# TensorE kept in the source's order through an attention stage, with one head's last products moved between the next head's scores

## The chip, the cores and the metric

The kernel runs on one core of a Trainium2 chip. The metric is device time in microseconds (us) of one execution. Three runs of the kernel before the change took 1217.46, 1221.15 and 1222.93 us; the median, 1221.15 us, is the time that is compared.

## The reference

One decoder layer over 1024 positions of width 1024: RMSNorm and one input projection, whose columns feed a short gated convolution, a stick-breaking attention and a chunked spatial gating; an output projection; a squared-ReLU MLP of width 4096; a gated per-layer embedding. The change touches the attention alone:

```
q = rms_norm(q, q_norm_g); k = rms_norm(k, k_norm_g)      # 8 heads of 64
for each block of 128 queries:
    z = q k^T / 8;  causal = key < query
    log_beta = log_sigmoid(z);  log_rem = where(causal, log_sigmoid(-z), 0)
    suffix = reverse cumulative sum of log_rem over keys, without the key itself
    weights = where(causal, exp(log_beta + suffix), 0)
    o = weights v
```

The kernel takes the suffix as a running product: rem = sigmoid(-z) is scanned from the last key to the first, and the weight is sigmoid(z) times the scanned rem of the next key.

## The kernel before, in words

Every float32 product is done as three products of rounded parts (hi by hi, hi by lo, lo by hi). A part pair is made by `split`: ScalarE writes the hi part, VectorE the rest (lo).

The heads are worked in four pairs. `project(pr)` makes one pair's q, k and v: for each of 8 blocks t of 128 positions, 24 matmuls into one of two banks of the pool `ps_mm` (tile `qkv_ps`), then the chain that empties the bank: ScalarE's squares (`qk_sq`), VectorE's sum (`ss`), GpSimd's power (`rs`), VectorE's scaling of q and k (`qk`), ScalarE's hi part of v, VectorE's lo part of v. `turn_qk`, put off by `later`, transposes q and k of two blocks through a bank of `ps_tr` (3 banks) and splits them into QS, KH, KL.

`attend(pr)` has two generators for a step (head hh, group g of two query blocks t = 2g, 2g+1). `stick` makes the weights: for each t, one or two banks of `ps_z` (2 banks) of scores (tile `z`, up to 512 keys each), ScalarE's two sigmoids of each bank (`rem`, `wt`), VectorE's scan of `rem` over (t+1)*128 keys, and the product into `wt` (VectorE for t = 3, 5, 7, GpSimd else). `gather` multiplies them with v: per turn j, up to four transposes into a bank of `ps_tr` (`w_tr`), a split into `wT_hi` and `wT_lo`, and four matmuls into `av`; a turn's products come two turns after its transposes. `attention` runs `stick` of step i+1 and then `gather` of step i. The groups go 0, 1, 2, 3 for the first head of a pair and 3, 2, 1, 0 for the second, so that two steps with g = 3, the widest, follow each other in the middle of each pair.

`weave` draws alternately on `attention` and on a filler (`project` of the next pair, and with the last pair the convolution), by shares of units. The text order is not the order on the engines: the program is built with a scheduler that goes by estimated times and may issue any ready instruction of any engine ahead of others that it estimates late. Within an engine the order is then fixed, and semaphores are waited for in that order. `tc.issue_after(ins)` is a context that keeps what is written inside it behind `ins` on the engine of `ins`; it puts no wait into the program.

Of the kernel before, what the change touches and what calls it, by code (L numbers as in the profile page):

```python
# [32 lines left out]
def hybrid_block(ctx: ExitStack, tc: tile.TileContext, a: dict):  # L33
# [98 lines left out]

    last_hi, last_power = [None], [None]
# [27 lines left out]
    def product(ps, terms, first=True, last=True):  # L161


        for i, ((lh, ll), (rh, rl)) in enumerate(terms):
            nc.tensor.matmul(ps, lh, rh, start=first and i == 0, stop=False)  # L165
            nc.tensor.matmul(ps, lh, rl, start=False, stop=False)  # L166
            done = nc.tensor.matmul(ps, ll, rh, start=False, stop=last and i == len(terms) - 1)  # L167
        return done
# [16 lines left out]
    def mean_square(acc, s):  # L185


        ps = bank(ps_tr, "ms_ps")
        for t in range(4):
            nc.tensor.matmul(ps[:, 2 * t:2 * t + 2], acc[:, t * P:(t + 1) * P], ones[:, :2],  # L190
                             start=True, stop=True)
        ms = small.tile([P, 4], F32, tag=f"ms{s}", name=name("ms"), bufs=1)
        nc.vector.tensor_scalar(out=ms, in0=ps.rearrange("p (t two) -> p t two", two=2)[:, :4, 0],
                                scalar1=1.0 / D, scalar2=EPS, op0=ALU.mult, op1=ALU.add)
        r = small.tile([P, 4], F32, tag=f"r{s}", name=name("r"), bufs=1)
        power_mhalf(r, ms, 4)
        return ms, r

    def spread(r, R):

        diag = slot("diag", shape=(P, 4, P))
        nc.vector.tensor_tensor(
            out=diag, in0=ident.unsqueeze(1).broadcast_to([P, 4, P]),
            in1=r.unsqueeze(2).broadcast_to([P, 4, P]), op=ALU.mult)
        ps = bank(ps_tr, "R_ps")
        nc.tensor.matmul(ps, ones, diag.rearrange("p t c -> p (t c)"), start=True, stop=True)
        nc.scalar.copy(R, ps)
        return R
# [58 lines left out]
    def weave(first, first_total, second, second_total):  # L267


        done = [0, 0]  # L270
        while True:
            if done[0] * second_total <= done[1] * first_total:
                got = next(first, None)
                if got is None:
                    return
                done[0] += got
            else:
                done[1] += next(second, 1000)
# [57 lines left out]

    last_pool, last_act = [None], [None]
# [5 lines left out]
    def project(pr):  # L343
# [11 lines left out]
        for t in range(KT):  # L355
# [11 lines left out]
            for k0 in range(0, KT, 2):  # L367
# [3 lines left out]

            sq = half_tmp("qk_sq", (P, 4, HD + 1))
            nc.scalar.copy(sq[:, :, HD], ms1e[t].broadcast_to([P, 4]))
            nc.scalar.activation(sq[:, :, :HD], ps[:, :256].rearrange("p (h d) -> p h d", d=HD),
                                 AF.Square, scale=HD ** -0.5)
            ss = small.tile([P, 4], F32, tag="ss", name=name("ss"))
# [9 lines left out]
            if t % 2 == 0:  # L386
                V[t // 2] = slot("V", F32R, (P, 2, 2, 2, HD))
            v = V[t // 2][:, t % 2]
            split(ps[:, 256:].rearrange("p (h d) -> p h d", d=HD), v[:, :, 0], v[:, :, 1], scale=r1[t])
# [3 lines left out]
    def turn_qk(head, t, qk):  # L393

        QS, KH, KL, _, low_q = head
        th = t // 4
        tr = bank(ps_tr, "qk_tr")
        for i in range(2):
            for j in range(2):
                o = j * 256 + i * P  # L400
                nc.tensor.transpose(tr[:, o:o + P], qk[:, i, j * P:(j + 1) * P], ident)
        ws = slice((t % 4 - 1) * P, (t % 4 + 1) * P)

        split(tr[:, :256], QS[0][th][:, ws], low_q[th][:, ws], scale=gq)
        nc.scalar.activation(KH[0][th][:, ws], tr[:, 256:], AF.Copy, scale=gk)
        for hh, own in enumerate((lo_p, hi_p)):
            nc.vector.scalar_tensor_tensor(out=KL[hh][th][own, ws], in0=tr[own, 256:],
                                           scalar=gk[own], in1=KH[0][th][own, ws],
                                           op0=ALU.mult, op1=ALU.subtract)
# [11 lines left out]
    def attend(pr):  # L421
# [13 lines left out]
        def stick(hh, g):  # L435
            weights[hh, g] = []
            for t in (2 * g, 2 * g + 1):
# [5 lines left out]
                for kh in reversed(range(th + 1)):  # L443
# [3 lines left out]
                    nc.tensor.matmul(z, QS[hh][th][:, ts], KH[hh][kh][:, :n],  # L447
                                     start=True, stop=False)
                    nc.tensor.matmul(z, QS[hh][th][:, ts], KL[hh][kh][:, :n],
                                     start=False, stop=kh < th)  # L450
                    if kh == th:

                        nc.tensor.matmul(z[:, n - P:], ident_r, below, start=False, stop=True)
# [15 lines left out]
        def gather(hh, g):  # L469
# [5 lines left out]
            def turn(j):  # L475
# [4 lines left out]
                for kb in (2 * j, 2 * j + 1):  # L480
                    first = 0 if kb <= 2 * g else 1
                    parts.append((kb, n, first))
                    for i in range(first, 2):
                        nc.tensor.transpose(tr[:, n:n + P], wts[i][:, kb * P:(kb + 1) * P], ident)  # L484
# [6 lines left out]
            for j in range(-2, g + 1):  # L491
                if j + 2 <= g:
                    turned.append(turn(j + 2))
                    yield 2 * turned[-1][3] + 10
                if j < 0:
                    continue
                parts, hi, lo, _ = turned.pop(0)
                for kb, o, first in parts:
                    m = 256 - first * P
                    lhs = V[kb // 2][:, kb % 2, hh].rearrange("p two d -> p (two d)")  # L500
                    for part in (hi, lo):
                        nc.tensor.matmul(av[:, first * P:], lhs, part[:, o:o + m],  # L502
                                         start=kb == 0 and part is hi,
                                         stop=kb == 2 * g + 1 and part is lo)
                yield 8

            if yb is None:
                if both[0] is None:
                    both[0] = slot("y_both")
                t = both[0]  # L510
                nc.scalar.copy(t[:, (g % 2) * 256:(g % 2 + 1) * 256], av)
                if len(seen_g) % 2:
                    nc.gpsimd.dma_start(t[:HD], t[HD:], accum_op=ALU.add)
                    summed.append((y_dram[pr, g // 2, own], t))
                    both[0] = None
                seen_g.append(g)
                return
            low = half_tmp("av_lo")
            nc.scalar.copy(low[:HD], av[HD:])
            nc.vector.tensor_tensor(out=yb[g // 2][own, (g % 2) * 256:(g % 2 + 1) * 256],  # L520
                                    in0=av[:HD], in1=low[:HD], op=ALU.add)
# [3 lines left out]
    def attention():  # L525
# [5 lines left out]
        yield from parts[0][0](*steps[0][1:])  # L531
        for i, (pr, *step) in enumerate(steps):
            if i + 1 < len(steps):
                nxt, *ahead = steps[i + 1]
                if nxt not in parts:
                    parts[nxt] = attend(nxt)
                yield from parts[nxt][0](*ahead)
# [4 lines left out]
            if i % 2 == 1:  # L542
                parts[pr][2]()
# [12 lines left out]
    def gating():  # L556
# [26 lines left out]
        def turn_c(th, j, yc, y):  # L583
            tr = bank(ps_tr, "c_tr")
            for t in range(4):
                nc.tensor.transpose(tr[:, t * P:(t + 1) * P],
# [756 lines left out]
```

## Time and profile before

| | |
|---|---|
| median of three runs | 1221.15 us |
| the profiled execution | 1216.81 us, its span 1214.9 us |
| TensorE busy | 1191.8 us (98% of the span) |
| VectorE, ScalarE, GpSimd busy | 886.8, 629.1, 400.9 us |
| mean granted TensorE clock | 0.993 |

PE is TensorE, PEld its weight loads, DVE VectorE, ACT ScalarE, POOL GpSimd. In tables of windows each row is a stretch of the span with its length, each engine's busy time in it (in brackets the number of instructions), the granted TensorE clock as a share of full speed, and the use of the DMA engines. A matmul's record is longer than the step to the next one, since matmuls are pipelined: a busy PE is not yet a PE at its peak.

### The profile page before, as it was taken

Reading aid. Unit: us, or ns where it says so; the run is one execution under the profiler, and the core shown is the slowest. Engines: PE = TensorE matmul, PEld = TensorE weight load, DVE = VectorE, ACT = ScalarE, POOL = GpSimd, SP = SyncE. Lnnn points to the kernel's source line nnn. Section 1 sums busy time; section 2 is a strip of 40 time slices with the busy share of each in tenths; the row PEclk is TensorE's granted clock in tenths of the full one; section 3 lists DMA queues with packets and bytes.
Section 4 is the critical chain, followed back from the end, with each engine's and each line's share of the span. In section 5 each row is a group of like instructions: output and inputs, shape, how many; then the busy total and the mean of one; then the engine's idle time right before and its main releaser. Section 6 shows DMA issues by size and latency. Waiting matters only on the chain.

```text
span 1214.9 us, 17743 instructions
## 1 busy us (share of the span) xinstructions
PE 1191.8 (98%) x5852; PEld 1018.2 (84%) x5852; DVE 886.8 (73%) x1310; ACT 629.1 (52%) x1244; POOL 400.9 (33%) x408
## 2 busy tenths in 40 slices
PE   9999899999999999999999999999999999999997
PEld 7899899898988888888888888888888888888886
DVE  7846888988887657877878768787665556753597
ACT  7736767667764355744333333356443444546542
POOL 3324345365343312124453544421023301013412
PEclk9999999999999999999999999999999999999998
DMA  9602359999554786779999899778889985654857
GB/s 318 222 18 94 124 166 267 247 184 171 132 116 101 164 287 207 198 194 269 251 256 251 231 261 258 217 249 277 321 248 313 279 264 171 217 163 112 179 160 208
DMA packets 127964, 254.04 MB, mean 209 GB/s; under 512 B 14496, under 2 KB 22432, under 8 KB 127168
## 3 DMA queue, kind: packets, MB, share of 16 engines
q1 hardware_dynamic: 94992, 168.08, 41.8%
q0 software_dynamic: 27664, 57.05, 25.0%
q10 hardware_dynamic: 5216, 27.79, 6.4%
q8 instruction: 46, 0.75, 0.2%
q14 instruction: 46, 0.38, 0.1%
HBM read 192.30 MB, written 92.80 MB: 235 GB/s over the span
## 4 chain that ended last, share of the span: by engine, by line
PE 86%; DVE 5%; DMA 4%; POOL 1%; issue 1%; ACT 1%; SPq 0%; ACTq 0%; DVEq 0%; POOLq 0%
PE f_ps L812 25%; PE d_ps L812 25%; PE g_ps L812 6%; PE qkv_ps L165 3%; PE qkv_ps L166 3%; PE qkv_ps L167 3%; PE av L502 2%; PE w_tr L484 2%; DVE rem L459 1%; PE vu_ps L167 1%; PE vu_ps L166 1%; PE vu_ps L165 1%; PE o_ps L167 1%; PE o_ps L165 1%; PE o_ps L166 1%
## 5 line engine op out<-in xcount | busy, mean ns | idle before, releaser
L139 DVE TENSOR_TENSOR w_lo<-raw,w_hi 128x512 fp32r<-128x512 f32 x280 | 245.1, 879 | 88.1 <-ACT w_hi L138 86.4
L138 ACT CAST w_hi<-raw 128x512 fp32r<-128x512 f32 x280 | 171.9, 619 | 232.6 <-PE d_ps L812 112.6
L812 PE MATMUL f_ps<-hn_hi,w_hi 128*128 128x512 f32 x448 | 175.1, 392 | 0.0
L812 PE MATMUL d_ps<-f_hi,w_hi 128*128 128x512 f32 x448 | 174.8, 390 | 0.0
L812 PE MATMUL f_ps<-hn_lo,w_hi 128*128 128x512 f32 x448 | 174.7, 390 | 0.0
L812 PE MATMUL f_ps<-hn_hi,w_lo 128*128 128x512 f32 x448 | 174.5, 390 | 0.0
L812 PE MATMUL d_ps<-f_hi,w_lo 128*128 128x512 f32 x448 | 174.3, 389 | 0.0
L812 PE MATMUL d_ps<-f_lo,w_hi 128*128 128x512 f32 x448 | 174.3, 389 | 0.0
L459 DVE TENSOR_TENSOR_SCAN rem<-rem 128x128 f32<-128x128 f32 (+3 forms) x64 | 90.2, 1420 | 23.0 <-ACT rem L454 22.9
L812 PEld LDWEIGHTS f_ps<-hn_lo,w_hi 128*128 128x128 f32 x448 | 84.4, 188 | 17.9 <-issue 0.2
L812 PEld LDWEIGHTS f_ps<-hn_hi,w_hi 128*128 128x128 f32 x448 | 84.5, 189 | 17.6 <-issue 0.2
L812 PEld LDWEIGHTS f_ps<-hn_hi,w_lo 128*128 128x128 f32 x448 | 84.4, 188 | 17.7
L812 PEld LDWEIGHTS d_ps<-f_hi,w_hi 128*128 128x128 f32 x448 | 84.1, 188 | 17.7 <-issue 0.2
L812 PEld LDWEIGHTS d_ps<-f_lo,w_hi 128*128 128x128 f32 x448 | 84.1, 188 | 17.6 <-issue 0.2
L812 PEld LDWEIGHTS d_ps<-f_hi,w_lo 128*128 128x128 f32 x448 | 84.1, 188 | 17.5
L165 PE MATMUL qkv_ps<-whi,xn_hi 128*128 128x384 f32 x256 | 90.4, 353 | 0.1
L167 PE MATMUL qkv_ps<-whi,xn_lo 128*128 128x384 f32 x256 | 87.8, 343 | 0.0
L166 PE MATMUL qkv_ps<-wlo,xn_hi 128*128 128x384 f32 x256 | 87.6, 342 | 0.0
L139 DVE TENSOR_TENSOR f_lo<-raw,f_hi 128x512 fp32r<-128x512 f32 x112 | 77.0, 718 | 12.6 <-ACT f_hi L138 12.2
L138 ACT CAST f_hi<-raw 128x512 fp32r<-128x512 f32 x112 | 67.0, 620 | 28.9 <-DMA raw<-f_dram 25.9
L798 POOL TENSOR_TENSOR S<-S,sq 128x512 f32<-128x512 f32 x19 | 27.4, 1440 | 157.8 <-ACT sq L874 157.8
L174 POOL TENSOR_TENSOR rs<-ss,mhalf 128x4 f32<-128x4 f32 x32 | 40.1, 1253 | 83.1 <-DVE ss L377 83.1
(252 smaller groups left out, 2704.4 us busy)
## 6 DMA issues: line engine op xcount, KB each, us to landing
raw<-in_w_ff SPq DMA_DIRECT2D x148, 256.0 KB, 4.1
raw<-f_dram SPq DMA_DIRECT2D x112, 256.0 KB, 5.1
raw<-w_sums SPq DMA_DIRECT2D x64, 256.0 KB, 3.9
f_dram<-f SPq DMA_DIRECT2D x48, 256.0 KB, 4.0
f_dram<-t SPq DMA_DIRECT2D x48, 256.0 KB, 3.7
w_sums<-in_w_ff POOLq DMA_DIRECT2D x8, 1024.0 KB, 11.6
w_sums<-w_sums POOLq DMA_DIRECT2D x8, 1024.0 KB, 13.0
raw<-in_w_out SPq DMA_DIRECT2D x28, 256.0 KB, 3.9
```

What stands on the lines that cost most here:

```text
L138: last_hi[0] = nc.scalar.copy(hi, src)
L139: low.tensor_tensor(out=lo, in0=src, in1=hi, op=ALU.subtract)
L165: nc.tensor.matmul(ps, lh, rh, start=first and i == 0, stop=False)
L166: nc.tensor.matmul(ps, lh, rl, start=False, stop=False)
L167: done = nc.tensor.matmul(ps, ll, rh, start=False, stop=last and i == len(terms) - 1)
L174: last_power[0] = nc.gpsimd.tensor_tensor(out=out, in0=in_, in1=mhalf[:, :n], op=ALU.pow)
L459: nc.vector.tensor_tensor_scan(out=back, data0=back, data1=back, initial=1.0, op0=ALU.mult, op1=ALU.bypass)
L484: nc.tensor.transpose(tr[:, n:n + P], wts[i][:, kb * P:(kb + 1) * P], ident)
L502: nc.tensor.matmul(av[:, first * P:], lhs, part[:, o:o + m], start=kb == 0 and part is hi, stop=kb == 2 * g + 1 and part is lo)
L798: return eng.tensor_tensor(out=out, in0=x, in1=y, op=ALU.add)
L812: done = nc.tensor.matmul(bank, l, r, start=first and k == 0 and i == 0, stop=k == len(b) - 1 and i == 2, skip_group_check=True)
```

## The change

`matmul` and `transpose` are wrappers that note the last matmul written. `weave` issues each piece behind it, so that within the woven stretch TensorE's pieces keep the source's order. In `gather` a turn's products become a function, `multiply`; turns 0 and 1 are no longer multiplied behind the step's last transposes but put on a list `rest`, from which the next step's `stick` takes one after each piece of scores. In `project` the hi part of v is made first, ahead of `qk_sq`, and its lo part ahead of `ss`; in `turn_qk` ScalarE makes both hi parts before VectorE makes the lo parts. The instructions are the same in kind and number on every engine; their order changes.

```diff
+    last_mm = [None]
+    def matmul(*args, **kw):
+        last_mm[0] = nc.tensor.matmul(*args, **kw)
+        return last_mm[0]
...
         while True:
+            with tc.issue_after(last_mm[0].ins):
-            if done[0] * second_total <= done[1] * first_total:
-                got = next(first, None)
+                if done[0] * second_total <= done[1] * first_total:
+                    got = next(first, None)
...
             (project)
+            v = V[t // 2][:, t % 2]
+            ps_v = ps[:, 256:].rearrange("p (h d) -> p h d", d=HD)
+            nc.scalar.activation(v[:, :, 0], ps_v, AF.Copy, scale=r1[t])
             sq = half_tmp("qk_sq", (P, 4, HD + 1))
...
+            nc.vector.scalar_tensor_tensor(out=v[:, :, 1], in0=ps_v, scalar=r1[t], in1=v[:, :, 0],
+                                           op0=ALU.mult, op1=ALU.subtract)
             ss = small.tile([P, 4], F32, tag="ss", name=name("ss"))
...
-            split(ps[:, 256:].rearrange("p (h d) -> p h d", d=HD), v[:, :, 0], v[:, :, 1], scale=r1[t])
...
             (turn_qk)
-        split(tr[:, :256], QS[0][th][:, ws], low_q[th][:, ws], scale=gq)
+        nc.scalar.activation(QS[0][th][:, ws], tr[:, :256], AF.Copy, scale=gq)
         nc.scalar.activation(KH[0][th][:, ws], tr[:, 256:], AF.Copy, scale=gk)
+        nc.vector.scalar_tensor_tensor(out=low_q[th][:, ws], in0=tr[:, :256], scalar=gq,
+                                       in1=QS[0][th][:, ws], op0=ALU.mult, op1=ALU.subtract)
...
             (gather)
-            for j in range(-2, g + 1):
-                if j + 2 <= g:
-                    turned.append(turn(j + 2))
-                    yield 2 * turned[-1][3] + 10
...
+            for j in range(g + 1):
+                *parts, n = turn(j)
+                turned.append(parts)
+                yield 2 * n + 10
+                if j > 1:
+                    multiply()
+                    yield 8
+            rest.extend([multiply] * len(turned))
...
             (attention)
+        def weights(nxt, *step):
+            for units in parts[nxt][0](*step):
+                yield units
+                if rest:
+                    rest.pop(0)()
+                    yield 8
...
-                yield from parts[nxt][0](*ahead)
+                yield from weights(*steps[i + 1])
+            while rest:
+                rest.pop(0)()
+                yield 8
```

How this moves instructions is shown at three places of the second pair, around its two steps with g = 3. A name ends in its buffer's number, and the same tile can have another number in the two programs.

On TensorE, before, at the scores of the second g = 3 step for t = 7:

```order
L447 MATMUL z_3523<-KH_2699,QS_2698 128x512
L449 MATMUL z_3523<-KL_2693,QS_2698 128x512
L453 MATMUL z_3523<-below,ident 128x128
L447 MATMUL z_3529<-KH_2287,QS_2698 128x512
L449 MATMUL z_3529<-KL_2281,QS_2698 128x512
L484 MATMUL w_tr_3544<-ident,wt_3397 128x128
L484 MATMUL w_tr_3544<-ident,wt_3376 128x128
L484 MATMUL w_tr_3544<-ident,wt_3397 128x128
L484 MATMUL w_tr_3553<-ident,wt_3397 128x128
L484 MATMUL w_tr_3553<-ident,wt_3376 128x128
L484 MATMUL w_tr_3553<-ident,wt_3397 128x128
L447 MATMUL z_3644<-KH_2699,QS_2698 128x128
```

On TensorE, now, at the same scores (z_3516 and z_3522 are what z_3523 and z_3529 were):

```order
L136 MATMUL z_3516<-KH_2689,QS_2688 128x512
L136 MATMUL z_3516<-KL_2683,QS_2688 128x512
L136 MATMUL z_3516<-below,ident 128x128
L136 MATMUL z_3522<-KH_2286,QS_2688 128x512
L136 MATMUL z_3522<-KL_2280,QS_2688 128x512
L136 MATMUL qkv_ps_3472<-whi_3121,xn_hi_264 128x384
```

The scores were followed by transposes of the weights just made and by further scores; now six matmuls of the filler (one qkv row is shown) stand behind them, four products of the step before, and then transposes and filler by turns.

On TensorE, now, the end of that run, the third turn's transposes and the first products of the step (wT_hi_3548 is the first turn's):

```order
L136 MATMUL qkv_ps_3571<-whi_3127,xn_lo_298 128x384
L140 MATMUL w_tr_3593<-ident,wt_3348 128x128
L140 MATMUL w_tr_3593<-ident,wt_3390 128x128
L140 MATMUL w_tr_3593<-ident,wt_3348 128x128
L140 MATMUL w_tr_3593<-ident,wt_3390 128x128
L136 MATMUL av_87<-wT_hi_3548,V_2380 128x256
L136 MATMUL av_87<-wT_lo_3549,V_2380 128x256
```

Between z_3522 and this av row stand 18 qkv matmuls, 4 products and 12 transposes.

On ScalarE, before, where the hi parts of v of two blocks are made (qkv_ps_3365 and qkv_ps_3473, the banks that the filler needs again):

```order
L454 ACTIVATE rem_3500<-z_3508 128x512
L455 ACTIVATE wt_3501<-z_3508 128x512
L405 ACTIVATE KH_3166<-qk_tr_3451,c_gk 128x256
L141 ACTIVATE V_3470<-qkv_ps_3365,r_569 128x2x64
L511 COPY y_both_3498<-av_87 128x256
L454 ACTIVATE rem_3521<-z_3523 128x512
L455 ACTIVATE wt_3522<-z_3523 128x512
L141 ACTIVATE V_3470<-qkv_ps_3473,r_569 128x2x64
```

On ScalarE, now, at the second of these blocks (qkv_ps_3472):

```order
L472 ACTIVATE rem_3514<-z_3522 128x512
L473 ACTIVATE wt_3515<-z_3522 128x512
L388 ACTIVATE V_3460<-qkv_ps_3472,r_569 128x2x64
L392 ACTIVATE qk_sq_3553<-qkv_ps_3472 128x4x64
L528 COPY y_both_3539<-av_87 128x256
L148 CAST wT_hi_3548<-w_tr_3543 128x512
```

The hi part of v stood behind two steps' sigmoids; now it stands directly ahead of the squares of its own bank.

On VectorE, before, at the same place:

```order
L459 SCALAR_TENSOR_TENSOR rem_3500<-rem_3500 128x896
L407 SCALAR_TENSOR_TENSOR KL_3162<-qk_tr_3451,c_gk,KH_3166 64x256
L407 SCALAR_TENSOR_TENSOR KL_3164<-qk_tr_3451,c_gk,KH_3166 64x256
L142 SCALAR_TENSOR_TENSOR V_3470<-qkv_ps_3365,r_569,V_3470 128x2x64
L142 SCALAR_TENSOR_TENSOR V_3470<-qkv_ps_3473,r_569,V_3470 128x2x64
L459 SCALAR_TENSOR_TENSOR rem_3521<-rem_3521 128x1024
L139 TENSOR_TENSOR wT_lo_3550<-w_tr_3544,wT_hi_3549 128x512
L462 TENSOR_TENSOR wt_3522<-wt_3522,rem_3521 128x1023
```

On VectorE, now (a row SCALAR_TENSOR_TENSOR rem<-rem is the scan):

```order
L477 SCALAR_TENSOR_TENSOR rem_3483<-rem_3483 128x896
L477 SCALAR_TENSOR_TENSOR rem_3514<-rem_3514 128x1024
L394 SCALAR_TENSOR_TENSOR V_3460<-qkv_ps_3472,r_569,V_3460 128x2x64
L397 TENSOR_REDUCE ss_3557<-qk_sq_3553 128x4
L480 TENSOR_TENSOR wt_3515<-wt_3515,rem_3514 128x1023
L149 TENSOR_TENSOR wT_lo_3549<-w_tr_3543,wT_hi_3548 128x512
L149 TENSOR_TENSOR wT_lo_3584<-w_tr_3578,wT_hi_3583 128x512
L402 TENSOR_TENSOR qk_3470<-qkv_ps_3472,rs_3559 128x256
```

The two lo parts of v, which ended the use of both banks, stood together between the two wide scans; now each bank ends with its own qk row, and the first lo part of the weights (wT_lo_3549) stands behind the widest scan and its product.

More of the change, by code (lines that the diff above doesn't have):

```diff
@@ L542, in attention @@
             if i % 2 == 1:
+                parts[pr][2]()
+            if i == len(steps) - 1:
+                while rest:
+                    rest.pop(0)()
+                    yield 8
                 parts[pr][2]()
```

92 lines of the change are left out of this document (47 added, 45 removed).

## The prediction

> **What bounds the kernel now.** First the page, for the whole span; then the windows of the attention stage; then PE's waits; then single instructions there.
>
> ```profile
> PE 1191.8 (98%) x5852; PEld 1018.2 (84%) x5852; DVE 886.8 (73%) x1310; ACT 629.1 (52%) x1244; POOL 400.9 (33%) x408
> ACT V L141 <- DVE qk L382: 22.0, 15, 2.6
> ```
>
> PE is busy 98% of the span, so a reordering of the same instructions can win only where PE waits or runs at a lower clock. The second line is a row of the list of waits; it is used below. The change moves instructions in the attention stage, about 113 to 375 us, which I cut into the middle of each of the first three head pairs (the two steps with g = 3) and the rest:
>
> ```profile
> core 0: us, PE busy (x) PEld busy (x) DVE busy (x) ACT busy (x) POOL busy (x), PEclk, DMA share, GB/s
> 113.00:134.00 21.00, 19.69 (x122) 18.91 (x121) 17.16 (x29) 14.61 (x40) 12.36 (x13) 1.00 0.56 182
> 134.00:151.00 17.00, 14.13 (x86) 12.03 (x86) 15.14 (x19) 13.42 (x33) 6.29 (x6) 0.98 0.39 132
> 151.00:202.50 51.50, 51.50 (x340) 50.73 (x340) 43.23 (x71) 35.06 (x91) 25.77 (x27) 0.97 0.73 207
> 202.50:219.50 17.00, 14.31 (x89) 12.46 (x87) 15.21 (x19) 13.10 (x32) 9.17 (x8) 0.97 0.84 221
> 219.50:272.00 52.50, 51.71 (x341) 50.72 (x340) 44.72 (x72) 34.51 (x91) 25.86 (x28) 0.98 0.93 220
> 272.00:288.50 16.50, 13.71 (x84) 11.55 (x82) 14.10 (x17) 13.17 (x33) 10.27 (x9) 1.00 0.81 143
> 288.50:375.00 86.50, 84.62 (x502) 74.62 (x503) 76.11 (x112) 54.54 (x127) 40.78 (x32) 1.00 0.69 142
> ```
>
> The reader is to see three short windows in which PE runs 84 to 89 matmuls in about 17 us, between long ones with 340 in 51.5 us. There PE idles while DVE is busy 85 to 89%; in the long windows PE has no idle time and DVE is busy only 84 or 85%. The work is the same in sum, but badly mixed: the middles are short of PE work, the rest of DVE work.
>
> ```profile
> PE w_tr L484 <- DVE KL L407: 4.6, 3, 1.7
> PE w_tr L484 <- DVE wt L462: 2.8, 4, 1.2
> PE z L447 <- ACT wt L455: 2.4, 7, 0.7
> PE av L502 <- DVE wT_lo L139: 1.6, 3, 0.9
> ```
>
> These waits of PE (us in total, times, longest) are for VectorE above all. Why the filler, which needs little of VectorE, did not fill them, single instructions tell:
>
> ```profile
> 138.43 0.42 DVE L382 TENSOR_TENSOR qk<-qkv_ps,rs 128x256 f32<-128x256 f32 x1 [1.14 <-POOL rs L174]
> 146.93 0.64 ACT L141 ACTIVATE V<-qkv_ps,r 128x128 fp32r<-128x128 f32 x2
> 150.26 0.61 DVE L142 SCALAR_TENSOR_TENSOR V<-qkv_ps,r,V 128x128 fp32r<-128x128 f32 x2
> 150.29 1.11 PE L484 MATMUL w_tr<-ident,wt 128*128 128x128 f32 x4 [1.14 <-DVE KL L407]
> 151.06 0.67 PE L165 MATMUL qkv_ps<-whi,xn_hi 128*128 128x384 f32 x1
> ```
>
> VectorE has scaled q and k of a bank at 138.8, but ScalarE reads v of the same bank only at 146.9 and VectorE at 150.3, together with the next bank's; the filler's next matmul runs at 151.1. That bank was held 8 us by the place of v in ScalarE's queue.
>
> **The change, part by part.** Parts one and two go together: v is read first, and PE keeps the text order. The bank is then ended by `qk`. No instruction is added; what goes is the hold, and the first windows' lack of PE work. Its worth: at the long windows' pace, 51.5/340 = 0.1515 us a matmul, 86 and 89 matmuls take 13.0 and 13.5 us instead of 17.0; at 52.5/341 = 0.154, 84 take 12.9 instead of 16.5. That is 4.0 + 3.5 + 3.6 = 11.1 us. To it comes a slower clock behind two of them:
>
> ```profile
> 147.00:150.30 3.30, 1.43 (x10) 1.07 (x10) 3.24 (x5) 3.30 (x10) 0.79 (x1) 0.99 0.00 0
> 150.30:154.00 3.70, 3.70 (x14) 3.70 (x15) 3.70 (x5) 0.93 (x2) 0.98 (x1) 0.54 0.00 0
> 218.70:222.00 3.30, 3.30 (x12) 3.30 (x13) 3.30 (x4) 0.60 (x2) 1.98 (x2) 0.51 1.13 208
> 284.00:288.50 4.50, 2.19 (x12) 1.39 (x12) 4.44 (x7) 4.36 (x12) 2.43 (x4) 1.00 1.13 208
> 288.50:292.00 3.50, 3.50 (x22) 3.50 (x23) 3.50 (x4) 0.59 (x1) 3.06 (x3) 1.00 1.13 207
> ```
>
> The granted clock is 0.54 for 3.7 us and 0.51 for 3.3 us: 3.7 x 0.46 + 3.3 x 0.49 = 3.3 us lost. The third middle is followed by full clock. In all 14.4 us can be won at the middles.
>
> [...]
>
> Against this stand new waits. In the text order a step's products stand at a fixed distance behind its transposes, and these behind the next step's scores. I walk through the second g = 3 step of a pair by the new order, from the end of its last scores (z_3522). The durations:
>
> ```profile
> 268.46 0.17 PE qkv_ps L166
> 269.44 0.35 PE av L502 x3
> 270.73 0.23 PE z L449
> 139.39 0.87 PE w_tr L484 x8
> L454 ACT ACTIVATE rem<-z 128x512 f32<-128x512 f32 x47 | 28.9, 614 | 16.9 <-PE z L449 15.3 <-PE z L453 1.0
> L455 ACT ACTIVATE wt<-z 128x512 f32<-128x512 f32 x47 | 29.0, 617 | 0.0
> L459 DVE TENSOR_TENSOR_SCAN rem<-rem 128x1024 f32<-128x1024 f32 x8 | 21.1, 2642 | 0.0
> L142 DVE SCALAR_TENSOR_TENSOR V<-qkv_ps,r,V 128x128 fp32r<-128x128 f32 x27 | 9.1, 347 | 3.0 <-ACT V L141 2.6
> L377 DVE TENSOR_REDUCE ss<-qk_sq 128x4 f32<-128x260 f32 x27 | 11.1, 412 | 2.8 <-ACT qk_sq L374 2.7
> L462 DVE TENSOR_TENSOR wt<-wt,rem 128x1023 f32<-128x1023 f32 x8 | 10.1, 1265 | 0.1
> L139 DVE TENSOR_TENSOR wT_lo<-w_tr,wT_hi 128x512 fp32r<-128x512 f32 x43 | 28.5, 680 | 2.9 <-ACT wT_hi L138 2.3
> ```
>
> PE has 18 filler matmuls of 0.173 us (3.1), 4 products (2 of 0.118 and 2 of half that, 0.4) and 12 transposes of 0.109 (1.3) to do until it wants wT_lo_3549: 4.8 us. VectorE can start the scan when ScalarE has done rem, wt, rem of the two banks, 1.85 us from a point 0.46 us (two z matmuls) before the end of the scores: at 1.4. Then stand on it the scan 2.64, v's lo part 0.35, ss 0.41, the product 1.27 and wT_lo 0.68: done at 6.75. PE waits about 2.0 us. The same walk for the first g = 3 step (18 filler matmuls, 4 products of 0.118, 15 transposes: 5.2 us; on VectorE 1.4 + 2.64 + 1.27 + 0.68 = 6.0) gives 0.8 us. So 2.8 us a pair, 8.3 us for three. In the fourth pair the filler is the convolution, whose matmuls are longer, and I take no such wait there.
>
> Score banks: the text order puts at least four matmuls of another kind between two uses of a `z` bank nearly everywhere. ScalarE needs 1.23 us for both sigmoids of a bank; the new order mostly leaves 1.4 us and more. Between a gain of the 2.4 us listed above and a loss of as much I take none.
>
> Outside the middles PE idles 21.00 - 19.69, 52.50 - 51.71 and 86.50 - 84.62 us, 4.0 in all. Part of it is transposes that wait for weights; in the new order a full step's `gather` and the next scores lie between weights and their transposes. I take half, 2.0 us; the ends are 0 and 4.0.
>
> `turn_qk`'s new order spares ScalarE a wait for VectorE, and the 22.0 us of ScalarE's waits for `qk` go too. ScalarE is busy 66 to 68% in the two windows of 340 matmuls and no bound there: nothing. The DMA issues of `block_sums` and `up_sums` keep their places behind the same steps; what they bring is used in the MLP, where the list of PE's waits has no row: nothing, and if they came late it would show there.
>
> Sum: 14.4 - 8.3 + 2.0 = 8.1 us. The profiled execution's 1216.81 us becomes 1208.7. It is 4.3 us under the median; taken from the median, 1221.15 - 8.1 = **1213 us**.
>
> **The rivals.** *VectorE bounds the stage.* It is busy 225.7 of 262 us (sum of the windows), 86%. My sum makes that 89%, the share that the middles have (15.14 of 17.00). A row shows that it can be fuller:
>
> ```profile
> 360.00:380.00 20.00, 18.81 (x104) 15.27 (x103) 19.19 (x25) 8.54 (x20) 12.03 (x7) 1.00 0.65 143
> ```
>
> That is 96%, so no ceiling stands in the way. But with a fixed order on every engine each late operand stops PE, and then VectorE's next input is late as well. If its share stays within 86 to 87%, the gain is 0 to 3 us: 1218 to 1221 us. Chance 0.24.
>
> *No new waits.* The scans may be done earlier than in my walk:
>
> ```profile
> 143.28 2.29 DVE L459 TENSOR_TENSOR_SCAN rem<-rem 128x1024 f32<-128x1024 f32 x1
> L459 DVE TENSOR_TENSOR_SCAN rem<-rem 128x768 f32<-128x768 f32 x8 | 14.1, 1758 | 7.4 <-ACT rem L454 7.4
> ```
>
> If the 2.29 us of this wide scan (mean 2.64) and shorter queues are the rule, all 14.4 + 2.0 us stay: 1204.7 us. With the whole 4.0, 1202.7. Chance 0.22.
>
> *Slower: the products of every wide step wait.* The place is `av` behind `wT_lo` as in my walk, but at all scans of 768 keys and more (three sizes, 8 each, 24), since PE can no longer pass over a late product. It decides from 16.4/24 = 0.68 us each: beyond it the kernel is slower. At 1.0 us: 24.0 - 16.4 = 7.6 us slower, 1229 us. Against it: a 768 scan (1.76 us) is shorter than the one in my walk by 0.9 us, and its first wT_lo stands ahead of its product. Chance 0.13.
>
> That the order on PE does not change is excluded by the rows shown.
>
> **How the numbers follow.** My forecast, gains of 5 to 12 us, 1209 to 1216 us: chance 0.41. A measurement of this kernel tells about 0.5% (6.1 us) from no change, so faster is below 1215.0 and slower above 1227.3. Faster: 0.22 and 0.35 of the 0.41, 0.57. Same: 0.24 and 0.06, 0.30. Slower: 0.13. The range takes in the full gain below and the VectorE rival above, 1202 to 1224 us, with what is slower left out.
>
> **What would show it.** Right: ScalarE's hi part of v follows its bank's last matmul within a us or two, also in the middles; no stretch at half clock in the stage; the waits of w_tr for KL and wt nearly gone; waits of `av` for wT_lo risen from 1.6 to some 8 us, behind the 1024 scans. The middles would be no longer told from the rest by matmuls per us. Wrong: if PE's waits for VectorE sum to what they were, spread over the pair (the first rival), or if `av` waits behind the 640 and 768 scans too (the last).

## The result, and the profile after

The changed kernel took 1248.82 us (median of four runs, 1246.12 to 1250.25) beside 1219.31 us for the kernel before in the same session: ratio 1.0238, 95% interval 1.0202 to 1.0275. It is 29.5 us slower, where 1213 us was predicted. The profiled execution took 1249.23 us with a span of 1247.1 us, 32.2 us more than before.

The first lines of its page:

```profile
span 1247.1 us, 17768 instructions
PE 1203.1 (96%) x5852; PEld 1029.0 (83%) x5852; DVE 889.5 (71%) x1310; ACT 630.3 (51%) x1244; POOL 403.0 (32%) x408
PEclk9999998898999999999999999999999999999999
```

TensorE is idle 1247.1 - 1203.1 = 44.0 us instead of 1214.9 - 1191.8 = 23.1, and the clock row falls below 9 at two places. The same windows as before (length, then PE, PEld, DVE, ACT and POOL busy with their counts, the granted clock, the DMA share, GB/s):

```profile
113.00:134.00 21.00, 16.80 (x92) 15.46 (x91) 15.82 (x28) 15.72 (x39) 11.46 (x12) 0.92 0.51 175
134.00:151.00 17.00, 15.94 (x103) 15.14 (x103) 14.27 (x15) 11.18 (x28) 7.46 (x5) 1.00 0.47 140
151.00:202.50 51.50, 42.67 (x275) 40.65 (x274) 39.34 (x61) 29.35 (x78) 24.45 (x25) 0.95 0.51 138
202.50:219.50 17.00, 16.97 (x92) 16.29 (x92) 13.99 (x19) 12.92 (x31) 5.57 (x4) 0.85 1.00 323
219.50:272.00 52.50, 46.89 (x291) 44.47 (x290) 37.49 (x57) 29.56 (x73) 22.14 (x20) 0.93 0.64 157
272.00:288.50 16.50, 14.57 (x86) 13.87 (x85) 14.65 (x25) 11.64 (x33) 13.57 (x15) 0.90 0.88 187
288.50:375.00 86.50, 77.89 (x465) 70.97 (x464) 69.49 (x104) 54.19 (x133) 32.92 (x32) 0.96 0.75 148
```

The three middles no longer stand out: 275 matmuls in 51.5 us is the pace of 92 in 17. But it is the long windows that came down to the middles. Where PE idled 4.0 us in the four windows outside the middles, it now idles 4.20 + 8.83 + 5.61 + 8.61 = 27.3 us, and VectorE is less busy too (39.34 of 51.50 instead of 43.23): both wait, by turns. The windows are cut at fixed times, so the later ones hold somewhat earlier work than before. The list of PE's waits (us in total, times, longest) names what it waits for:

```profile
PE av L136 <- DVE wT_lo L149: 10.6, 11, 2.2
PE qk_tr L140 <- DVE qk L402: 7.5, 4, 2.5
PE qkv_ps L136 <- DVE qk L402: 6.8, 4, 2.2
PE w_tr L140 <- DVE wT_lo L149: 3.2, 2, 2.4
PE R_ps L136 <- DVE diag L212: 2.8, 1, 2.8
PE w_tr L140 <- DVE KL L425: 1.5, 1, 1.5
PE z L136 <- ACT wt L473: 0.6, 1, 0.6
```

The largest cause, 14.3 us in two rows, is `qk`, the last step of the chain that empties a bank; before, no row of the list was for it. Single instructions on three engines show why it is late. They are block 10's (block 2 of the second pair), from its last product to its `qk`, in order of time; the sixth row, at 156.67, is the next block's high part of v:

```profile
146.10 0.33 PE L136 MATMUL qkv_ps<-whi,xn_lo 128*128 128x384 f32 x1
150.75 0.51 ACT L421 ACTIVATE KH<-qk_tr,c_gk 128x256 fp32r<-128x256 f32 x1
151.11 0.41 ACT L388 ACTIVATE V<-qkv_ps,r 128x128 fp32r<-128x128 f32 x1
151.36 0.43 ACT L392 ACTIVATE qk_sq<-qkv_ps 128x256 f32<-128x256 f32 x1
153.69 0.41 DVE L397 TENSOR_REDUCE ss<-qk_sq 128x4 f32<-128x260 f32 x1
156.67 0.37 ACT L388 ACTIVATE V<-qkv_ps,r 128x128 fp32r<-128x128 f32 x1 [0.47 <-PE qkv_ps L136]
157.16 0.42 DVE L402 TENSOR_TENSOR qk<-qkv_ps,rs 128x256 f32<-128x256 f32 x1 [0.86 <-POOL rs L184]
```

The bank is complete at 146.43, but the high part of v is read only at 151.11, behind the KH of the turning before it, and the squares, which before stood ahead of v, now stand behind it. `qk` begins 10.7 us after the last product (before: 4.4). Of these 6.3 us, 4.2 stand ahead of the squares; the rest is in the chain behind them, where GpSimd's power took 2.95 us (before 1.03). The odd block after it is read as soon as its products end (it waited for PE). It is so all through the stage: in blocks 8 to 31 the even ones are read 1.7 to 6.3 us after their last product, but for block 24, and the odd ones 0 to 0.4 us, but for block 29 (1.2). `qk` begins up to 14.6 us after the last product, before at most 7.6.

The second part of the loss is the clock. Windows of the same kernel, around two single waits of 2.03 and 2.19 us, for `qk` and for wT_lo:

```profile
104.70:107.00 2.30, 0.40 (x3) 0.08 (x1) 1.43 (x5) 0.93 (x4) 1.28 (x2) 1.00 0.00 0
107.00:108.70 1.70, 1.57 (x9) 1.60 (x10) 0.42 (x1) 0.00 (x0) 0.74 (x1) 0.96 0.00 0
108.70:111.70 3.00, 3.00 (x11) 3.00 (x10) 0.00 (x0) 0.00 (x0) 0.00 (x0) 0.50 0.00 0
156.80:159.30 2.50, 0.39 (x4) 0.18 (x2) 2.14 (x4) 0.98 (x3) 1.36 (x3) 1.00 0.00 0
159.90:163.00 3.10, 3.10 (x13) 3.00 (x13) 1.62 (x5) 0.52 (x2) 1.01 (x1) 0.50 0.00 0
```

After each, PE runs some 3.4 us at half clock, a loss of 1.7 us on top of the wait. Windows of half a microsecond from 60 to 380 us show nine such stretches, one of them twice as long, against two before; summed, (1 - clock) x length is 17.1 us against 3.4, 13.7 us more. Elsewhere the changed kernel lost less to the clock than before: over the whole span the mean granted clock is 0.984 instead of 0.993, which makes 1247.1 x 0.016 - 1214.9 x 0.007 = 11.4 us. With 20.9 us more idle time that is 32.3 for a span that grew by 32.2. All of it lies in the attention stage: its last product with v ends at 443.7 us instead of 408.7, and the kernel's end keeps most of these 35 us.

### The profile page after: what moved, and what is told of

Its sections match the earlier page's. It is cut to its first block, busy times and chain, and to the rows that moved or that the text cites. A ratio compares the mean times of both kernels' runs of the same rounds, so it can differ in the third digit from the quotient of the medians.

```text
span 1247.1 us, 17768 instructions
## 1 busy us (share of the span) xinstructions
PE 1203.1 (96%) x5852; PEld 1029.0 (83%) x5852; DVE 889.5 (71%) x1310; ACT 630.3 (51%) x1244; POOL 403.0 (32%) x408
## 4 chain that ended last, share of the span: by engine, by line
PE 87%; DVE 7%; issue 2%; ACT 2%; POOL 1%; DMA 0%; ACTq 0%; SPq 0%; DVEq 0%; POOLq 0%
PE f_ps L854 24%; PE d_ps L854 24%; PE qkv_ps L136 7%; PE o_ps L136 7%; PE g_ps L854 6%; PE cv_ps L136 5%; PE vu_ps L136 4%; DVE rem L477 2%; PE av L136 2%; PE z L136 2%; PE pp_ps L136 2%; PE w_tr L140 1%; DVE wT_lo L149 1%; ACT rem L472 1%; DVE wt L480 1%
## 5 line engine op out<-in xcount | busy, mean ns | idle before, releaser
L149 DVE TENSOR_TENSOR w_lo<-raw,w_hi 128x512 fp32r<-128x512 f32 x280 | 241.2, 865 | 90.3 <-ACT w_hi L148 88.3
L477 DVE TENSOR_TENSOR_SCAN rem<-rem 128x128 f32<-128x128 f32 (+3 forms) x64 | 93.4, 1460 | 38.7 <-ACT rem L472 38.3
L136 PE MATMUL qkv_ps<-whi,xn_hi 128*128 128x384 f32 x256 | 95.1, 372 | 6.8 <-DVE qk L402 6.8
L480 POOL TENSOR_TENSOR wt<-wt,rem 128x127 f32<-128x127 f32 (+4 forms) x40 | 43.8, 1097 | 117.8 <-DVE rem L477 76.0
```

Of the source, the lines that this page charges most:

```text
L136: last_mm[0] = nc.tensor.matmul(*args, **kw)
L149: low.tensor_tensor(out=lo, in0=src, in1=hi, op=ALU.subtract)
L477: nc.vector.tensor_tensor_scan(out=back, data0=back, data1=back, initial=1.0, op0=ALU.mult, op1=ALU.bypass)
L480: done = (nc.vector if on_vector else nc.gpsimd).tensor_tensor(out=wt[:, :W - 1], in0=wt[:, :W - 1], in1=rem[:, 1:W], op=ALU.mult)
```

## The experiments

The change has three parts: the fixed order on TensorE (`issue_after` in `weave`), the last products between later scores (`rest`, `multiply`), and banks first (`project` and `turn_qk`). Nothing is left out of a kernel here unless it is said. The kernel before, run beside them, had medians between 1217.34 and 1218.95 us. Each expectation numbers its theories for itself.

**One part alone, and the change without its order.** The parts are those of the diff above, each put into the kernel before, or the first taken out of the change.

The fixed order alone:

> Kernel before with one part of the change alone: weave issues each piece behind the last matmul written, so TensorE keeps the text order; products with v, v's split and turn_qk as before. Theory 1 (the fixed order itself costs: TensorE can no longer pass over a late product of VectorE): 1240 to 1255 us, TensorE waits for VectorE over 15 us, stretches at half clock in the stage. Theory 2 (the new place of v and qk in VectorE's and ScalarE's queues costs): within 6 us of before, 1214 to 1227. Theory 3 (the products between later scores cost): the same as theory 2.

The products' place alone:

> Kernel before with the second part alone: a step's last two products with v come between the next step's scores; the scheduler is free to move them. Theory 1: within 6 us of before (1214 to 1227), since nothing is held in order. Theory 2: the same. Theory 3: slower by 10 us or more, with av waiting for wT_lo.

Banks first alone:

> Kernel before with the third part alone: ScalarE reads the shared banks first (v's hi part ahead of the squares, both hi parts of q and k ahead of the lo parts), the scheduler free. Theory 1: faster than before by 3 to 12 us (1208 to 1217), the hold of the filler's bank by v gone, no new waits. Theory 2: slower by 8 us or more, TensorE waiting for qk as in the changed kernel (14.3 us there). Theory 3: as theory 1.

The change without the fixed order:

> The changed kernel without the fixed order: products between later scores and ScalarE first, but weave no longer issues behind the last matmul. Theory 1: not slower than before, 1206 to 1222 us, TensorE's waits for qk and wT_lo back under 5 us in all. Theory 2 and theory 3: slower than before by 8 us or more, up to the changed kernel's 1249.

Measured: 1268.95 us (ratio 1.0426, 1.041 to 1.0441), 1217.18 us (0.9996, 0.9981 to 1.0011), 1233.58 us (1.0131, 1.0114 to 1.0148) and 1225.98 us (1.0071, 1.0055 to 1.0087). So the order is dear, dearer than its theory 1 had it. Banks first, which the prediction had free the middles together with the order, costs 16 us by itself, and the change without the order is 8.6 us slower. For these two the time is theory 2's, though banks first alone waits only 3.0 us for `qk`. PE's largest waits, first with the order alone, then with banks first alone:

```profile
PE av L136 <- DVE wT_lo L149: 26.3, 25, 2.1
PE qk_tr L140 <- DVE qk L394: 5.4, 3, 3.8
```

```profile
PE av L136 <- DVE wT_lo L149: 10.6, 6, 2.1
PE w_tr L140 <- DVE wt L480: 4.6, 3, 1.5
PE z L136 <- ACT wt L473: 3.3, 4, 2.1
```

With the order alone, 25 products with v wait behind their own transposes. That is what the place of the products is for, and what the next run tests.

**The other pairs, VectorE relieved, and ScalarE's sigmoids held behind the banks.**

The order with the products' place:

> The changed kernel without the third part: fixed order on TensorE and products between later scores, but v's split and turn_qk as before. The fixed order alone took 1269, all three parts 1249. If the products between later scores are what eases the fixed order (a longer way from transposes to products, so fewer of the 26.3 us that av waits for wT_lo): about 1249 or less, 1235 to 1252. If the early reading of the banks eases it: 1262 to 1272.

The order with banks first:

> The changed kernel without the second part: fixed order on TensorE and ScalarE first, but a step's last two products directly behind its transposes. If the products' place eases the fixed order: 1262 to 1280, av waiting for wT_lo over 20 us. If the early reading eases it: 1240 to 1252.

The changed kernel with one line changed:

```diff
-                on_vector = t in (3, 5, 7)
+                on_vector = False
```

> The changed kernel with the products wt times rem of t = 3, 5, 7 on GpSimd instead of VectorE (22 instructions, 23.5 us of VectorE's work in the stage, less). If TensorE waits for VectorE's queue: waits for wT_lo and qk fall by a half or more and the kernel takes 1228 to 1240 us. If it waits for the chain through the scan whatever VectorE's load: the same or slower, 1245 to 1262, as GpSimd takes some 2 us for a product that VectorE does in 1.27.

Banks first alone, with the sigmoids issued behind the last bank's squares (`last_v` notes these):

```diff
+                    with tc.issue_after(last_v[0].ins):
                         nc.scalar.activation(rem[:, ks], z, AF.Sigmoid, scale=-HD ** -0.5)
```

> The third part alone (1233.6 us, the hold of the filler's banks there 17 to 24 us in the middles) with one more order: ScalarE's sigmoids of later scores are issued behind the hi part of v and the squares of the last block written. TensorE is free. If the hold of the bank in ScalarE's queue is what the middles lose: hold under 9 us, faster than before, 1205 to 1214 us. If VectorE's backlog is what the middles lose and the bank only shows it: no gain, 1216 to 1235.

Measured: 1234.37 us (1.0143, 1.0126 to 1.016), 1282.97 us (1.0529, 1.0498 to 1.056), 1233.96 us (1.0137, 1.0121 to 1.0152) and 1228.27 us (1.0088, 1.0072 to 1.0103). The eight combinations of the parts, in us (the first is the median beside the first four runs):

| | without the order | with the order |
|---|---|---|
| neither | 1217.3 | 1269.0 |
| products' place | 1217.2 | 1234.4 |
| banks first | 1233.6 | 1283.0 |
| both | 1226.0 | 1248.8 |

Banks first costs 9 to 16 us wherever it is added; the order 17 to 52 us; the products' place is worth nothing alone, 8 us with banks first, and 34 to 35 us where the order is fixed. Relieving VectorE of 24 products (23.2 us in the changed kernel) gives back 15 us. Its waits:

```profile
PE qk_tr L140 <- DVE qk L402: 7.4, 4, 2.5
PE qkv_ps L136 <- DVE qk L402: 7.3, 4, 2.0
PE av L136 <- DVE wT_lo L149: 5.0, 5, 1.4
```

The waits for wT_lo fell from 13.8 to 6.2 us (with 1.2 us at the transposes), those for `qk` not at all: 14.7 us instead of 14.3. Of the gain, 8.1 us are idle time, and the rest goes with the granted clock (0.991 instead of 0.984). So VectorE's load explains the waits for wT_lo, not those for `qk`. Holding back the sigmoids got 5 of the 16 us back, and v of even blocks stayed late (9.6 us at block 10): the sigmoids are not the main reason.

**Why v is late in even blocks.** The tile V is new in even blocks, and takes a slot of the pool `sp` with its first write, the high part. In the text, the turning of the block pair before stands directly ahead of it and takes slots too (`q_lo`, `QS`, `KH`). In the built program of banks first alone the slots are taken in that order: in nine of the twelve even blocks 8 to 30 the first write of V follows directly on that of `q_lo` or `QS`, though five to eight slots stood free. Banks first alone, around block 10, on ScalarE:

```profile
150.59 0.38 ACT L388 ACTIVATE V<-qkv_ps,r 128x128 fp32r<-128x128 f32 x1
150.86 0.40 ACT L392 ACTIVATE qk_sq<-qkv_ps 128x256 f32<-128x256 f32 x1
```

There the products had ended at 137.5: 13.1 us. Four kernels make the first write of V an early one, ahead of the block's products, with one tiny instruction on GpSimd for every two blocks:

```diff
+            if t % 2 == 0:
+                V[t // 2] = slot("V", F32R, (P, 2, 2, 2, HD))
+                nc.gpsimd.memset(V[t // 2][:, 0, 0, 0, :1].bitcast(F32), 0.0)
             ps = bank(ps_mm, "qkv_ps")[:, :384]
...
-            if t % 2 == 0:
-                V[t // 2] = slot("V", F32R, (P, 2, 2, 2, HD))
             v = V[t // 2][:, t % 2]
```

Banks first alone with it:

> Banks first alone, with the tile V of each even block written once at the head of its block (GpSimd sets one column to 0, which takes the slot of the pool there), so that V's turn at the pool no longer comes behind the tiles that the turning of the block before takes. One instruction more per two blocks, nothing left out. Theory 1 (the pool hands out its slots in the order of the text, so V's high part of an even block stood behind VectorE's first write of q_lo or of QS, and the squares, sums and qk behind it): the high part follows the last product of even blocks within about 2 us also in the middles (now 13.1, 11.7 and 10.7 us at blocks 10, 18 and 26), the 14 us that banks first cost in every combination are gone, 1210 to 1220 us, and if the prediction's middles exist at all they show here, down to 1205. Theory 2 (reading the bank for v first is itself dear, since it delays the sigmoids on ScalarE and other work on VectorE): no change, 1230 to 1236.

The changed kernel with it:

> The changed kernel with the same early write of V. Nothing left out. Theory 1: it loses the 14 us that banks first added to the other two parts (1234.4 without banks first), so 1228 to 1236 us, or below if banks read first now help; its waits of TensorE for qk (14.3 us in two rows) fall below 5 us. Theory 2: no change, 1246 to 1252.

The change without the order, with it:

> Banks first and the products between later scores, without the fixed order, with the early write of V. Nothing left out. Theory 1: the 8.6 us over the products alone are gone, 1205 to 1218 us. Theory 2: 1224 to 1228.

The kernel before with it:

> The kernel before with the early write of V and nothing else; here the squares already stand ahead of V. Theory 1: V's high part loses its place behind the turning, but stays behind the sigmoids that ScalarE's order puts ahead of it; the banks come free earlier in part, 1210 to 1218 us. Theory 2: the place of v does not matter while the squares go first, 1216 to 1220, the same as before.

Measured: 1211.53 us (0.9945, 0.9926 to 0.9964), 1240.37 us (1.0178, 1.016 to 1.0196), 1207.34 us (0.9908, 0.9885 to 0.9931) and 1210.31 us (0.9936, 0.9914 to 0.9958). Without the order all three are faster than the kernel before, and 1207.34 us is the fastest kernel of this study. Banks first alone falls by 22 us. Its block 10 and its three middles:

```profile
137.07 0.33 PE L136 MATMUL qkv_ps<-whi,xn_lo 128*128 128x384 f32 x1
137.82 0.37 ACT L389 ACTIVATE V<-qkv_ps,r 128x128 fp32r<-128x128 f32 x1 [0.17 <-issue]
```

```profile
134.00:151.00 17.00, 17.00 (x108) 16.48 (x107) 12.28 (x17) 10.46 (x27) 7.90 (x9) 1.00 0.41 140
202.50:219.50 17.00, 17.00 (x110) 16.40 (x109) 13.14 (x18) 11.11 (x28) 8.27 (x9) 1.00 0.81 201
272.00:288.50 16.50, 16.50 (x108) 15.83 (x107) 14.45 (x19) 12.35 (x29) 10.71 (x12) 1.00 0.91 162
```

V is read 0.4 us after the last product, and PE has no idle time in the windows of the middles: 108, 110 and 108 matmuls where there were 86, 89 and 84. Not all blocks became prompt; blocks 8, 14 and 16 stay 7 to 10 us late. And the kernel before with the early write alone (1210.31) is as fast as banks first with it (1211.53): what helped was V's turn at the pool, and the order of the reads had nothing to add. The kernel before with it, in the same windows:

```profile
134.00:151.00 17.00, 16.81 (x108) 15.99 (x107) 14.29 (x17) 11.57 (x29) 6.84 (x6) 1.00 0.33 125
202.50:219.50 17.00, 17.00 (x110) 16.45 (x109) 13.23 (x18) 11.11 (x28) 8.83 (x9) 1.00 0.86 194
272.00:288.50 16.50, 16.50 (x107) 15.83 (x107) 13.94 (x18) 11.20 (x28) 8.55 (x9) 1.00 0.88 156
```

There v is still read late on the whole, but at blocks 10, 18 and 26, those of the middles, 3.8 to 5.6 us after the last product instead of 12.0 to 12.9. A rival, that any small edit turns the scheduler's choices to the better, was not tested by a write at another place; against it stands that all four kernels gained, by 8 to 22 us.

The changed kernel gained 8 us only, not the 14 expected. Its lateness of v is gone (0.0 to 0.8 us in all even blocks but block 16, 1.8), and so are the filler's waits for `qk`; those of the transposes (`qk_tr`) are 10.8 us. They are 10.1 us in the order with the products' place too, so they come with the order and not with banks first.

**What the fixed order costs.** With V early the order still takes 1207.34 to 1240.37 us, 33 us. The stage in the two, first without and then with it, and PE's waits with it:

```profile
113.00:375.00 262.00, 255.80 (x1606) 238.20 (x1605) 231.12 (x343) 180.77 (x454) 131.72 (x134) 0.99 0.74 182
```

```profile
113.00:375.00 262.00, 232.82 (x1421) 217.46 (x1420) 213.93 (x307) 166.23 (x411) 118.84 (x124) 0.95 0.69 168
```

```profile
PE qk_tr L140 <- DVE qk L403: 10.8, 3, 5.0
PE av L136 <- DVE wT_lo L149: 8.7, 10, 1.5
PE w_tr L140 <- DVE wT_lo L149: 3.8, 2, 2.4
PE w_tr L140 <- DVE KL L426: 2.6, 1, 2.6
```

Over the whole span the idle time differs by 23.3 us (42.0 against 18.7) and the busy time by 7.5 (1196.9 against 1189.4); the clock, summed as above from 60 to 380 us, by 10.2 (11.9 against 1.7). Three runs asked where it comes from. The turning put 108 units behind its block instead of 72:

> The changed kernel with V claimed early (1240.4 us), and the turning of q and k placed 108 instead of 72 units of filler behind the block, half a block later in TensorE's fixed order. Nothing left out. Theory 1 (the fixed order costs what single results come late by, so a result given more room costs nothing): the three waits for qk at the turning (10.8 us, and most of the half clock behind them) are gone, 1224 to 1232 us. Theory 2 (VectorE's queue bounds the stage, so that TensorE waits for it at the next place instead): the waits move to the products with v and the turning of the weights, 1237 to 1243.

`issue_after` around the filler's pieces only:

> The changed kernel with V claimed early; a piece of the filler is issued only behind the last matmul of the text before it, a piece of attention is free. Nothing left out. Theory 1: attention may run ahead of filler whose qk is late, but the filler still stands behind late products with v; the 10.8 us for qk go, the 15 us for wT_lo and KL stay, 1222 to 1232 us. Rival: the order costs only where attention is tied, 1205 to 1212. Other rival: it costs only where the filler is tied, 1236 to 1244.

and around attention's pieces only:

> The counterpart of the run before: a piece of attention is issued only behind the last matmul of the text before it, a piece of the filler is free and may run ahead into the waits of attention. Nothing left out. Theory 1: the waits for wT_lo and KL (15 us) are filled with products of the filler, those for qk stay, 1218 to 1228 us. Rival (the order costs only where the filler is tied): 1205 to 1212. Other rival (only where attention is tied): 1236 to 1244.

A fourth run, without the order, relieved VectorE as above:

> Banks first and products between later scores with V claimed early, without the fixed order (1207.3 us), and the product with wt of the blocks 3, 5 and 7 on GpSimd instead of VectorE (23.5 us of VectorE's work moved). Nothing left out. If VectorE's queue still holds TensorE here: 1202 to 1206. If TensorE is the bound (its waits in the stage are under 3 us): 1206 to 1209, the same. If GpSimd's slower product becomes the late one: 1210 to 1216.

Measured: 1244.29 us (1.0218, 1.0187 to 1.0249), 1224.79 us (1.0064, 1.0043 to 1.0085), 1218.94 us (1.0013, 0.9998 to 1.0027), 1226.3 us (1.0072, 1.0044 to 1.01). The first missed: the waits for `qk` stayed, since the three long ones stand at the starts of the pairs, where the last turning is put directly behind its block whatever the number says. Tying one side alone costs 17 us (filler) or 12 us (attention), together 29, near the 33 of both. With one side free, the 10.8 us for `qk` at the transposes are 0.9 us or less. So neither kind of late result is the cause by itself. The reading that fits these runs is that the cost lies in TensorE no longer going past a late one on either side. The fourth run moved work to GpSimd without the order and lost; its runs spread from 1214.89 to 1230.67 us and the profile is of the lowest, with this among PE's waits:

```profile
PE qkv_ps L136 <- DVE qk L403: 3.8, 2, 2.9
PE w_tr L140 <- POOL wt L481: 2.1, 1, 2.1
```

GpSimd's late product has a row, but 2.1 us is not the 19 us between the medians; what slowed the other runs stays open.

**Room for the last turnings.** The last two runs give the turnings at the pairs' starts room:

```diff
-        while waiting:
+        while len(waiting) > 1:
             emitted[0] += waiting.pop(0)[1]()
+        waiting[:] = [(emitted[0] + 36, piece) for _, piece in waiting]
```

(and the same for the stretch ahead of the first pair). They do more than was intended: in the second, third and fourth pair the scores of the first head's query block 4, and in the second and third of block 5 too, read q and k ahead of the turning's last copies, so these scores are computed from other operands, and the copies wait for them.

> The changed kernel with V claimed early (1240.4 us), and the turning of each pair's last two blocks no longer put directly behind the products but 36 units of filler into the next pair. Nothing left out. Theory 1 (the fixed order costs what single results come late by at places without room): the waits of 4.4, 5.2 and 1.9 us for qk at the starts of the first three pairs are gone, and of the half clock behind each about 1.6 us, 1224 to 1231 us. Theory 2 (VectorE's queue bounds the stage, TensorE waits for it at the next place): 1236 to 1243.

> The same later turning in the kernel without the fixed order (banks first, products between later scores, V claimed early, 1207.3 us). Nothing left out. Theory 1: without the fixed order TensorE already passes the late turning (its wait there is 0.4 us), so nothing changes, 1204 to 1210. Rival: the later turning delays the scores behind it, 1211 to 1216.

Measured: 1244.8 us (1.0243, 1.0209 to 1.0276) and 1221.92 us (1.0032, 1.0016 to 1.0049). Among PE's waits in the first of them:

```profile
PE z L136 <- DVE QS L435: 20.3, 4, 7.4
PE av L136 <- DVE wT_lo L149: 8.0, 7, 2.4
PE qk_tr L140 <- DVE qk L403: 1.4, 1, 1.4
```

The waits for `qk` are gone as intended (10.8 to 1.4 us), and 20.3 us of waits of the scores for the same turning's last copy have come. They are one at the start of each pair. The first pair is not touched by the other operands: there the wait for `qk` went from 4.2 to 1.4 us, and one of 4.6 us for QS came. So in that pair the room given to the one result moved the wait to the next one out of VectorE's queue; for the other three, and for the second run as a whole, nothing can be concluded.

## Why the prediction was wrong, step by step

*The middles are short of TensorE work, and 14.4 us can be won there.* Right in kind. With V's slot taken early and the order free, PE is all but full in the three windows, without a stretch of half clock there. These three kernels gained 7 to 12 us of the 14.4.

*The hold is "the place of v in ScalarE's queue", and reading v first releases it.* This is the first step that failed. The rows were read rightly; the cause of the place was not looked for. At the blocks that hold the middles it is V's turn at the pool, and moving the read forward in the text does not bring that turn forward: at block 10 the high part came 12.9 us after the last product before, 13.1 us with banks first alone, and still 4.7 us in the changed kernel. Odd blocks, whose V has its slot already, are read at once. Worse, the squares, and with them `ss`, `rs` and `qk`, moved behind it. Instead of 14.4 us won, 9 to 16 us were lost in every combination of the table. That V's first write matters was shown by moving it alone; that the slots go by the text's order is inferred from the built program.

*New waits, 8.3 us.* This is the second step that failed, a term of the right kind and too small. `av` behind wT_lo went from 1.6 to 10.6 us. In the first pair the two walked waits came as forecast (1.06 and 2.19 us; the walk had 0.8 and 2.0), in the next two only one of them each (1.53 and 0.81), and 4.1 of the 10.6 us stand behind scans of fewer keys: that the row's total met the forecast is partly luck. The walk was made at two places of a pair, and for one kind of result. The order makes TensorE wait for every late result of VectorE: 14.3 us for `qk`, 3.2 us for wT_lo at the transposes, 2.8 us for `diag` in the convolution. With V early the order costs 33 us, four times the term; some 7 to 10 of them are the clock.

Counted by the table, the two steps are the whole miss: without the order the other two parts cost 8.7 us where 14.4 were to be won, and the order adds 22.8 us where 8.3 - 2.0 were forecast, 23.1 and 16.5 us off.

*No price for the clock.* The prediction counted half clock as lost before and won back, and gave the new waits none. In the stage 13.7 us more were lost to it. The stretches are 3.4 us long, one of them twice that, and waits of 1.53 to 2.84 us went ahead of them.

*Outside the middles PE's 4.0 us of idle time halve.* Wrong by sign: 27.3 us.

*The score banks, nothing; w_tr's waits for KL and wt nearly gone.* Right: 2.4 to 0.6 us for the first, 7.4 to 1.5 us for the second. The DMAs: right, no row of PE's waits names one. `turn_qk`'s own reordering was not run apart from `project`'s, and stays open.

*The rivals.* "VectorE bounds the stage" had the mechanism of a late operand that stops PE, after which VectorE's next input is late as well, and kept the time at 1218 to 1221 us. VectorE's share did not stay but fell, to 205 of the 262 us (sum of the windows): with fixed orders both engines can wait, by turns. The slower rival had the right cause, "PE can no longer pass over a late product", and stopped at one kind of product: it gave 1229 us. With the order alone `av` waits as it said, 25 times and 1.05 us each, and that kernel is 52 us slower, so even there the waits of `av` are half of it.

## What to carry to other kernels

Where a read is late in a queue, find out what put it there before moving it in the text: here a new tile's turn at a shared pool, which one tiny early write for every two blocks mended for 8 us, and a reordering made worse. When an engine that could pass a late operand is tied to the text, price every late operand of the stretch and not the one in view; a scheduler's freedom was worth 17 to 52 us here. Put half clock beside the price of TensorE's waits, as a term that may come: in the changed kernel single waits of 1.80 to 2.84 us cost 1.7 us on top, while with the order alone, and with banks first alone and V early, waits of 2.1 to 2.4 us were followed by full clock.

## What the runs showed of the hardware

In the changed kernel a single wait of TensorE of 2.03 us (from 105.1 us) was followed by 3.4 us at a granted clock of 0.50 (from 108.6 us). Between 60 and 400 us its nine longest waits, 1.80 to 2.84 us, were followed so, 2.6 to 3.8 us after they began where they stood alone, and one of 1.53 us at 225.5 us; two of the nine stretches stand behind two waits close together, and one of these is twice as long (6.8 us from 200.7 us). The other single waits, 0.20 to 1.46 us and one of 1.55 us at 253.8 us, were followed by full clock.

The length of a wait alone does not tell it. In windows of half a microsecond full clock also followed waits of 2.4 us at 124.0 us (banks first alone with V early; full until 333 us) and, with the order alone, of 2.1 us at 137.0 us (full until 152 us) and 2.4 us at 257.2 us (full until 302 us).
